# A hybrid encoder block in float32 pieces on one core: memory pools in another order, and tiles at multiples of 128 bytes

## The chip, the core and the metric

The kernel runs on one core of a Trainium2 chip. Its engines have a queue of instructions each: TensorE (PE, with the loading of the stationary operand, "PEld", as a queue that runs beside its matmuls), VectorE (DVE), ScalarE (ACT), GpSimd (POOL) and SyncE (SP), which issues all of this kernel's DMA transfers. The on-chip memory has 128 partitions; a tile is a stretch of bytes at the same address in each of them. The metric is the device time in microseconds (us) of one execution; lower is better.

## What is computed

One layer of a residual block over 1024 frames of 1024 values, and a last RMS norm. Group A is a gated linear recurrence in chunks of 64 frames (4 heads), group B a short gated convolution.

```python
h = rmsnorm(x, norm_gain[l])
proj = jnp.einsum('bsd,dc->bsc', h, w_in[l])          # 1024 x 1024 times 1024 x 4096
q, f_logit, i_in, z_a, u, gate_b, gate_c, z_b = jnp.split(proj, splits, axis=-1)
f = lb + (1.0 - lb) * jax.nn.sigmoid(f_logit.astype(jnp.float32))
o_a = hgrn2_chunkwise(q.reshape(hs), jnp.log(f).reshape(hs), (1.0 - f).reshape(hs), i_in.reshape(hs))
o_a = grouped_rmsnorm(o_a.reshape(bsz, s, D_HGRN), hgrn_norm_gain[l], HGRN_HEADS) * jax.nn.silu(z_a)
y_b = gate_b * causal_depthwise_conv(gate_c * u, conv_w[l])
o_b = grouped_rmsnorm(y_b, conv_norm_gain[l], CONV_GROUPS) * jax.nn.silu(z_b)
x = x + jnp.einsum('bsc,cd->bsd', jnp.concatenate([o_a, o_b], axis=-1), w_out[l])
return rmsnorm(x, final_norm_gain)
```

## The kernel before

**Matmuls.** Every large operand is split into a high part in float32r and a low part, the rest (lines 153 to 155, 301 to 315 and 662 to 664: a cast on ScalarE, a subtraction on VectorE). A product of two such operands is three matmuls: high by high, high by low, low by high. A matmul has a stationary operand of 128 x 128 and a moving one of 128 x 512.

**Stages.** First the value projection (lines 233 to 240, tiles `pv`), for two halves of the frames: stationary is a slice of x in XH or XL, moving are the weights of block k. For k below 4 these weights stand in XH and XL too (line 159), for k from 4 on in tiles `wvh` and `wvl` of the pools hip and lop (lines 161 and 162). Then 14 pairs of weight blocks (line 291): the first two pairs with 8 plain products each (tile `p`), the other 12 with 7 products each, by a Strassen-like scheme (tiles `pa`, `pb`, `pd`, `pe`). `product` (lines 335 to 343) issues 12 matmuls: stationary is a slice of the weights' high or low part (`hB`, `lB`, `hT`, `lT`, in the pools hip and lop), moving is a slab of XH or XL:

```python
pe.mm(ps, wh_[:, c], XH[:, a, k, :], start=(first and k == 0), stop=False, **more)
pe.mm(ps, wh_[:, c], XL[:, a, k, :], start=False, stop=False, **more)
pe.mm(ps, wl_[:, c], XH[:, a, k, :], start=False, stop=(last and k == 3), **more)
```

Last comes the output projection (`out_mms`, lines 794 to 804, tile `po`), in two halves of the output's columns: stationary is the mixed result in XH or XL, moving are the output weights. In the first half six of the eight blocks of weights stand in hip and lop (`woh`, `wol`, line 747) and two in XH and XL; in the second half all stand in XH and XL (line 743). The last tile is done in two pieces of 256 columns.

**Order.** All five queues are written by hand. A counter of the large matmuls (class `Stream`) places the other engines' work and the small float32 matmuls between them: scores and state updates of the recurrence (lines 477, 478, 491, 493, 494), the convolution's norm (602, 609), transposes (212, 681). So each engine's order is fixed by the code.

**Memory.** A pool takes its place when it is opened, in the order of lines 93 to 99; inside `const`, tiles follow one another in the order in which they are made, each rounded up to 32 bytes. `const` stands first and holds XH, XL, `vo` (values and later results), `mb`, `ident`, `mask` and the score tiles `sc`, with small tiles between them; the other pools begin where it ends.

Of the kernel before, what the change touches and what calls it, by code (L numbers as in the profile page):

```python
# [9 lines left out]
F32 = mybir.dt.float32  # L10
# [6 lines left out]
P = 128  # L17
# [3 lines left out]
NT = S // P  # L21
# [67 lines left out]
def hybrid_block(ctx: ExitStack, tc: tile.TileContext, xT, x, wv, wpair, wout, cols, fgain, out):  # L89
    nc = tc.nc  # L90
    A, V, G, T = nc.scalar, nc.vector, nc.gpsimd, nc.tensor

    const = ctx.enter_context(tc.tile_pool(name="const", bufs=1))
    hip = ctx.enter_context(tc.tile_pool(name="hip", bufs=NHL))
    lop = ctx.enter_context(tc.tile_pool(name="lop", bufs=NHL))
    rawp = ctx.enter_context(tc.tile_pool(name="rawp", bufs=6))
    tmp = ctx.enter_context(tc.tile_pool(name="tmp", bufs=8))
    qk = ctx.enter_context(tc.tile_pool(name="qk", bufs=2))
    sm = ctx.enter_context(tc.tile_pool(name="sm", bufs=2))
    dram = ctx.enter_context(tc.tile_pool(name="dram", bufs=2, space=bass.MemoryType.DRAM))  # L100
    psa = ctx.enter_context(tc.tile_pool(name="psa", bufs=1, space=PSUM))
# [17 lines left out]

    XH = const.tile([P, 7, 4, W], F32R, name="XH")  # L120
    XL = const.tile([P, 7, 4, W], F32R, name="XL")
    rst = const.tile([P, NT], F32, name="rst")
    vo = const.tile([P, NT, W], F32, name="vo")
    mb = const.tile([P, 4, S], F32, name="mb")
    col = const.tile([P, NCOL], F32, name="col")
    epsc = const.tile([P, 1], F32, name="epsc")
    ones = const.tile([P, 1], F32, name="ones")
    zeros = const.tile([P, 1], F32, name="zeros")
    ident = const.tile([P, P], F32, name="ident")

    pa = [bank_a(t, f"pv{t}") for t in range(4)]
    V.memset(zeros, 0.0)
# [110 lines left out]
        A.activation(vo[:, 4 * hf + t, :], p_, AF.Copy, scale=rst[:, 4 * hf + t:4 * hf + t + 1])  # L243


    mask = const.tile([P, P], F32, name="mask")
    G.memset(mask, 1.0)
    G.affine_select(out=mask, in_=mask, pattern=[[1, P]], compare_op=ALU.is_ge, fill=0.0, base=0,
                    channel_multiplier=-1)
# [1 line left out]
    G.memset(bones, 0.0)  # L251
    G.memset(bones[0:64, 0:1], 1.0 / 64)
    G.memset(bones[64:128, 1:2], 1.0 / 64)
    NS = 3
    scbuf = [const.tile([P, P], F32, name=f"sc{i}") for i in range(NS)]
    for s_ in scbuf:
        G.memset(s_, 0.0)

# [141 lines left out]
    def head(h):  # L400
# [71 lines left out]
        def scores(pr):  # L472
# [7 lines left out]
            pe.at(2, lambda: A.copy(kts[pr], psc[:, 1]),  # L480
                  lambda: V.copy_predicated(scbuf[(h * NT + pr) % NS], mask.bitcast(I32), psc[:, 0]))  # L481

        def combine(pr):
# [3 lines left out]
            vp = vo[:, pr, h * P:(h + 1) * P]  # L487
            sc, state = scbuf[(h * NT + pr) % NS], states.get(pr)
            po = psb.tile([P, 2, P], F32, tag="ps", name=f"po{n_}")
# [272 lines left out]
    for g, (n, step) in enumerate(products):  # L762
        if n == npair - 1:
            i = ORDER.index(step)
# [163 lines left out]
```

## Time and profile before

| | |
|---|---|
| device time, median of 3 runs | 470.25 us (469.73 to 570.84) |
| device time of the profiled execution | 469.7 us |
| its span, first to last instruction | 468.0 us |
| PE busy | 460.7 us (98%), 2200 matmuls |
| weight loads busy | 380.8 us |
| DVE, ACT, POOL busy | 326.6, 230.9, 101.8 us |
| moved by DMA | 40.83 MB |

The table is of one profiled execution. Matmuls overlap: each shows 0.39 to 0.48 us in the warm stretches, while a new one starts every 0.23 us or so. Their starts, not their durations, tell the pace.

### The profile page before, as it was taken

What the parts mean: (1) busy time and instruction counts of PE and PEld (TensorE: products, weight loads), DVE (VectorE), ACT (ScalarE), POOL (GpSimd) and SP (SyncE); (2) the same over time, 40 slices, a digit from 0 to 9 for tenths busy, and PEclk for the clock granted to TensorE, in tenths of its full rate; (3) what the DMA queues carried; (4) which work ended last, traced back from release to release, by engine and by line L of the source; (5) the groups of instructions that cost most, each with busy time, mean ns of one, the idle gap of its engine ahead of it and who ended that gap; (6) DMA issues with size and microseconds to landing.
All of it is one profiled execution on the core that took longest, in us unless ns stands there. A gap on an engine that the chain in (4) does not pass through costs nothing. (4 is left out here: it accounts for less than half of the span.)

```text
span 468.0 us, 6245 instructions
## 1 busy us (share of the span) xinstructions
PE 460.7 (98%) x2200; PEld 380.8 (81%) x2200; DVE 326.6 (70%) x593; ACT 230.9 (49%) x553; POOL 101.8 (22%) x92
## 2 busy tenths in 40 slices
PE   8999999999999999999999999999999999999995
PEld 7888888888888888888888888878888888888884
DVE  3668677989967789658799468798367796423333
ACT  5977415474454554454443545454646744314223
POOL 1100000005520053410326210326333343220000
PEclk9999999999999999999999999999999999999999
DMA  8990211120023020022020212020004228101442
GB/s 257 396 377 12 84 47 44 22 67 25 22 91 91 24 67 25 23 91 90 22 69 24 66 48 91 22 87 27 25 24 140 85 93 276 59 2 68 152 162 91
DMA packets 22031, 40.83 MB, mean 87 GB/s; under 512 B 2736, under 2 KB 2800, under 8 KB 22000
## 3 DMA queue, kind: packets, MB, share of 16 engines
q1 hardware_dynamic: 22000, 40.43, 26.2%
q8 instruction: 17, 0.28, 0.3%
q14 instruction: 14, 0.11, 0.1%
HBM read 36.19 MB, written 4.23 MB: 86 GB/s over the span
## 5 line engine op out<-in xcount | busy, mean ns | idle before, releaser
L314 DVE TENSOR_TENSOR lT<-T,hT 128x512 fp32r<-128x512 f32 x48 | 32.5, 677 | 32.8 <-ACT hT L313 32.5
L449 POOL TENSOR_TENSOR kh<-kh,ei 128x512 f32<-128x512 f32 x8 | 11.7, 1469 | 137.7 <-DVE ei L448 137.7
L60 PE MATMUL pb<-XH,lT 128*128 128x512 f32 x96 | 39.2, 408 | 0.0
L60 PE MATMUL pb<-XL,hT 128*128 128x512 f32 x96 | 38.7, 403 | 0.0
L60 PE MATMUL pb<-XH,hT 128*128 128x512 f32 x96 | 38.0, 396 | 0.0
L509 ACT COPY vo<-po 128x128 f32<-128x128 f32 x32 | 8.5, 266 | 54.6 <-DVE st L507 41.8
L313 ACT CAST hB<-B 128x512 fp32r<-128x512 f32 x44 | 27.6, 629 | 11.2 <-issue 11.1
L60 PE MATMUL po<-XH 128*128 128x512 f32 (+1 forms) x88 | 32.7, 372 | 0.0
L60 PE MATMUL po<-XH,XL 128*128 128x512 f32 (+1 forms) x88 | 32.7, 372 | 0.0
L60 PE MATMUL po<-XL,XH 128*128 128x512 f32 (+1 forms) x88 | 32.6, 370 | 0.0
L314 DVE TENSOR_TENSOR lB<-B,hB 128x512 fp32r<-128x512 f32 x44 | 32.2, 732 | 0.2 <-ACT hB L313 0.2
L313 ACT CAST hT<-T 128x512 fp32r<-128x512 f32 x48 | 28.4, 591 | 4.3 <-DVE T L305 4.3
L448 DVE RECIPROCAL ei<-e 128x128 f32<-128x128 f32 x32 | 29.5, 931 | 0.0
L60 PE MATMUL p<-XH,hB 128*128 128x512 f32 x64 | 25.3, 396 | 0.0
L60 PE MATMUL p<-XL,hB 128*128 128x512 f32 x64 | 25.3, 396 | 0.0
L60 PE MATMUL p<-XH,lB 128*128 128x512 f32 x64 | 25.3, 396 | 0.0
L60 PEld LDWEIGHTS pb<-XL,hT 128*128 128x128 f32 x96 | 18.0, 188 | 4.5 <-issue 0.3
L60 PEld LDWEIGHTS pb<-XH,hT 128*128 128x128 f32 x96 | 18.1, 188 | 4.1
L481 DVE COPY_PREDICATED sc<-mask,psc 128x128 f32<-128x128 int32 x32 | 9.6, 300 | 16.8 <-ACT kt L480 16.6
L60 PEld LDWEIGHTS pb<-XH,lT 128*128 128x128 f32 x96 | 18.1, 189 | 3.3
L60 PE MATMUL pe<-XL,hT 128*128 128x512 f32 x48 | 19.7, 410 | 0.0
L844 DVE TENSOR_TENSOR r<-po,xo 128x512 f32<-128x512 f32 (+1 forms) x9 | 5.7, 633 | 19.9 <-PE po L60 19.9
(217 smaller groups left out, 1367.8 us busy)
## 6 DMA issues: line engine op xcount, KB each, us to landing
B<-wpair SPq DMA_DIRECT2D x56, 256.0 KB, 2.6
wo<-wout SPq DMA_DIRECT2D x16, 256.0 KB, 3.0
xo<-x SPq DMA_DIRECT2D x16, 256.0 KB, 3.4
out<-y SPq DMA_DIRECT2D x16, 256.0 KB, 2.3
wv<-wv SPq DMA_DIRECT2D x8, 256.0 KB, 7.2
x<-xT SPq DMA_DIRECT2D x8, 256.0 KB, 6.2
vo<-x SPq DMA_DIRECT2D x4, 512.0 KB
mb<-xT SPq DMA_DIRECT2D x8, 256.0 KB, 5.9
```

The costliest lines, as they stand in the source:

```text
L60: self.T.matmul(*args, **kw)
L313: A.copy(hi, src)
L314: pe.at(5, lambda: V.tensor_tensor(lo, src, f32(hi), op=ALU.subtract))
L448: pe.at(9 + gap * i, lambda c0=i * P: V.reciprocal(eis[0][:, c0:c0 + P], e[:, c0:c0 + P]))
L449: pe.at(10 + 4 * gap - 3, lambda: G.tensor_tensor(kh, kh, eis[0], op=ALU.mult), lambda: G.tensor_tensor(ev[:, :, 0, :], ev[:, :, 0, :], ei ...
L481: lambda: V.copy_predicated(scbuf[(h * NT + pr) % NS], mask.bitcast(I32), psc[:, 0]))
L509: A.copy(vp, po[:, 0])
L844: V.tensor_tensor(r, po[:, c0:c1], xr[:, c0:c1], op=ALU.add)
```

## The change

Two things are put in another order: the pools (`const` is opened after hip, lop, rawp, tmp and qk instead of before them) and the tiles inside `const` (the large ones first, the small ones behind them; `ident`, `mask` and the three `sc` tiles move up).

```diff
-    const = ctx.enter_context(tc.tile_pool(name="const", bufs=1))
+
     hip = ctx.enter_context(tc.tile_pool(name="hip", bufs=NHL))
     lop = ctx.enter_context(tc.tile_pool(name="lop", bufs=NHL))
     rawp = ctx.enter_context(tc.tile_pool(name="rawp", bufs=6))
     tmp = ctx.enter_context(tc.tile_pool(name="tmp", bufs=8))
     qk = ctx.enter_context(tc.tile_pool(name="qk", bufs=2))
+    const = ctx.enter_context(tc.tile_pool(name="const", bufs=1))
     sm = ctx.enter_context(tc.tile_pool(name="sm", bufs=2))
...
     XL = const.tile([P, 7, 4, W], F32R, name="XL")
-    rst = const.tile([P, NT], F32, name="rst")
     vo = const.tile([P, NT, W], F32, name="vo")
     mb = const.tile([P, 4, S], F32, name="mb")
+    ident = const.tile([P, P], F32, name="ident")
+    mask = const.tile([P, P], F32, name="mask")
+    NS = 3
+    scbuf = [const.tile([P, P], F32, name=f"sc{i}") for i in range(NS)]
+    rst = const.tile([P, NT], F32, name="rst")
     col = const.tile([P, NCOL], F32, name="col")
...
-    ident = const.tile([P, P], F32, name="ident")
...
-    mask = const.tile([P, P], F32, name="mask")
...
-    NS = 3
-    scbuf = [const.tile([P, P], F32, name=f"sc{i}") for i in range(NS)]
```

The addresses in the two built programs, in bytes within a partition, and the offset of each from a multiple of 128:

| tiles | before | offset | after | offset |
|---|---|---|---|---|
| XH, XL | 384, 57728 | 0, 0 | 74112, 131456 | 0, 0 |
| hip (high parts) | 151232 to 163520 | 64 | 384 to 12672 | 0 |
| lop (low parts) | 163520 to 175808 | 64 | 12672 to 24960 | 0 |
| rawp, tmp, qk | 175808 to 224960 | 64 | 24960 to 74112 | 0 |
| vo, mb | 115104, 131488 | 32, 32 | 188800, 205184 | 0, 0 |
| ident, sc | 148128, 149280 | 32, 32 | 221568, 222592 | 0, 0 |
| mask | 148736 | 0 | 222080 | 0 |
| sm (`kt`, `st`, `dec`) | 225216 to 229312 | 64 | the same | 64 |

The instructions of all five queues, their order and their operands are the same in both programs, and so is which buffer of a pool each tile gets.

## Rows read from the trace of the kernel before

**Rows 1.** From the page: busy time of TensorE's two sides and VectorE, and granted clock.
```profile
PE 460.7 (98%) x2200; PEld 380.8 (81%) x2200; DVE 326.6 (70%) x593; ACT 230.9 (49%) x553; POOL 101.8 (22%) x92
PEclk9999999999999999999999999999999999999999
```
**Rows 2.** Who waited for whom, matmuls, then weight loads: us in total, times, longest.
```profile
PE pv L138 <- DVE epsc L133: 1.0, 1, 1.0
PE pv L60 <- ACT XH L179: 0.5, 1, 0.5
...
PEld pb L60 <- issue: 0.5, 3, 0.2
```
**Rows 3.** Timeline, the end: start, us taken, engine, line, what.
```profile
461.97 0.28 PE L60 MATMUL po<-XH,XL 128*128 128x256 f32 x1
...
464.83 0.37 SPq L866 DMA_DIRECT2D out<-y  x1
```
**Rows 4.** Timeline of TensorE's matmuls: first product, and the one after 192.
```profile
52.11 0.40 PE L60 MATMUL p<-XH,hB 128*128 128x512 f32 x1
...
96.91 0.40 PE L60 MATMUL pb<-XH,hB 128*128 128x512 f32 x1
```
**Rows 5.** The same, output projection's second half: first, and the one after 168.
```profile
418.24 0.40 PE L60 MATMUL po<-XH 128*128 128x512 f32 x1
...
456.34 0.28 PE L60 MATMUL po<-XH 128*128 128x256 f32 x1
```
**Rows 6.** The same, value projection, k below 4: one, and the 14th after it.
```profile
13.73 0.39 PE L60 MATMUL pv<-XL,XH 128*128 128x512 f32 x1
...
16.90 0.39 PE L60 MATMUL pv<-XH 128*128 128x512 f32 x1
```
**Rows 7.** The same, value projection, k of 4 and more: first, and the 41st after it.
```profile
18.26 0.40 PE L60 MATMUL pv<-wvh,XH 128*128 128x512 f32 x1
...
27.66 0.40 PE L60 MATMUL pv<-wvh,XL 128*128 128x512 f32 x1
```
**Rows 8.** Busy time by stretch: from and to, length, engines, granted clock, DMA, GB/s.
```profile
core 0: us, PE busy (x) PEld busy (x) DVE busy (x) ACT busy (x) POOL busy (x), PEclk, DMA share, GB/s
13.70:17.00 3.30, 3.30 (x16) 2.72 (x15) 1.42 (x3) 2.96 (x7) 0.00 (x0) 1.00 1.05 409
52.00:97.00 45.00, 45.00 (x195) 36.26 (x194) 35.18 (x58) 19.33 (x35) 0.00 (x0) 1.00 0.13 35
90.00:150.00 60.00, 60.00 (x289) 49.34 (x288) 52.05 (x97) 32.19 (x74) 15.43 (x12) 1.00 0.17 50
```
**Rows 9.** Timeline of TensorE around small matmuls, then their groups: busy us, mean ns.
```profile
129.14 0.38 PE L491 MATMUL po<-vo,kt 128*128 128x128 f32 x2
129.36 0.39 PE L494 MATMUL po<-vo,sc 128*128 128x128 f32 x2
129.50 0.48 PE L60 MATMUL pb<-XH,lT 128*128 128x512 f32 x1
129.82 0.39 PE L60 MATMUL pd<-XH,hB 128*128 128x512 f32 x1
...
L494 PE MATMUL po<-vo,sc 128*128 128x128 f32 x64 | 12.4, 275 | 0.0
L491 PE MATMUL po<-vo,kt 128*128 128x128 f32 x56 | 10.7, 273 | 0.0
L681 PE MATMUL pt<-ident,vo 128*128 128x128 f32 x32 | 4.8, 272 | 0.0
```
**Rows 10.** Groups of instructions by line: the split's subtraction into lop and into XL.
```profile
L155 DVE TENSOR_TENSOR wvl<-wv,wvh 128x512 fp32r<-128x512 f32 x4 | 2.8, 692 | 3.7 <-ACT wvh L154 3.7
L155 DVE TENSOR_TENSOR XL<-wv,XH 128x512 fp32r<-128x512 f32 x4 | 2.8, 690 | 4.7 <-ACT XH L154 4.7
```
**Rows 11.** Timeline: a low part on VectorE, and the load of it as weights.
```profile
176.00 0.63 DVE L314 TENSOR_TENSOR lT<-T,hT 128x512 fp32r<-128x512 f32 x1
...
183.01 0.19 PEld L60 LDWEIGHTS pb<-XH,lT 128*128 128x128 f32 x1
```

## What I predict

> **What bounds the kernel now.** The page comes first: of 468.0 us the matmul side of TensorE is busy 460.7, VectorE 326.6, and the granted clock is full in all 40 slices [rows 1]. A busy share can hide waiting, so the second view is the list of what TensorE's two sides waited for. Both rows of the matmul side lie in the first 6 us, and of the weight loads none waits more than 0.2 us after that [rows 2]. So from about 6 us to the last matmul at 461.97 [rows 3] the matmuls are issued as closely as the engine takes them, and the time is the sum of their distances from start to start. I write "step" for that distance. The third view is therefore the timeline of TensorE alone, of which only starts are read. Durations there are 0.39 to 0.40 us everywhere, overlap, and tell little.
>
> The step is not the same in all stages, although each stage shown here runs the same matmul (128 rows, 128 weights, 512 moving columns, float32r):
> - the products, tile `p`: 52.11 to 96.91 is 44.80 us over 192 matmuls, 233.3 ns [rows 4];
> - the second half of the output projection: 418.24 to 456.34 is 38.10 us over 168 matmuls, 226.8 ns [rows 5];
> - the value projection, k below 4: 13.73 to 16.90 is 3.17 us over 14, 226.4 ns [rows 6];
> - the value projection, k of 4 and more: 18.26 to 27.66 is 9.40 us over 41, 229.3 ns [rows 7].
>
> Now put addresses beside these. At 226 to 227 both operands lie in XH and XL, at a multiple of 128 bytes. At 229 the moving operand is `wvh`/`wvl` from hip and lop, 64 bytes off a multiple of 128, and the stationary one is aligned. At 233 the stationary operand is the one 64 off and the moving one is aligned. In code, products and output projection are alike: lines 341 to 343 and 802 to 804 issue three matmuls with the stationary operands a, a, b and the moving ones c, d, c, in long runs into one bank. Load by the other engines doesn't explain the difference: in 13.7 to 17 ScalarE is busy 2.96 of 3.30 us and the DMA engines all the time, at 226.4; in 52 to 97 ScalarE is busy 43% of the time and DMA 13%, at 233.3 [rows 8]. What is left is where the operands lie, and the change moves exactly that.
>
> **The change, part by part.** No instruction is added, removed or moved: on all five engines the order and the operands are those of before, so each term is a changed duration. All 512-column tiles come to multiples of 128.
>
> Stationary operands of the products. There are 2 x 8 x 12 + 12 x 7 x 12 = 1200 of these matmuls. 85 of them stand right behind a group of small matmuls (32 of scores, 32 of combine, 8 + 8 of the convolution's norm, 5 of the gate's transposes); the one in the rows takes 0.32 us to the next start [rows 9], and no aligned example exists in the products. The other 1115 go from 233.3 to 226.8: 6.5 ns each, 7.25 us. The 85 give between 0 and the same 6.5 ns, 0 to 0.55 us; I take the middle, 0.3. Together 7.55.
>
> Moving operands. 96 matmuls of the value projection (2 halves, 4 values of k, 4 tiles, 3 each) and 144 of the output projection's first half (8 tiles, 6 values of k, 3 each) read a moving tile that is 64 off: 229.3 - 226.8 = 2.5 ns each, 0.6 us.
>
> Small float32 matmuls. The records of lines 477, 478, 491, 493, 494, 602 and 681 whose operand gets a new offset are 64 + 32 + 56 + 56 + 64 + 64 + 32 = 368. They start 0.11 us apart [rows 9], and no aligned one is in the trace. Below: nothing. Above: the nearest row that prices a misplaced stationary operand, 6.5 ns each, 2.4 us. I stay near the lower end with 0.4 us, because their means of 272 to 275 ns don't part by the offset: in line 494 and line 681 the stationary tile is 32 off, in line 491 it is 64 off.
>
> VectorE, ScalarE and GpSimd. The split's subtraction takes 690 ns into aligned XL and 692 into `wvl` [rows 10]. So offsets cost these engines nothing that shows, and I set them to 0; were 1% lost there, it would lie under TensorE, since VectorE has 7.95 of 60 us free even in 90 to 150 [rows 8].
>
> DMA. Raw, x and y tiles are written or read at new offsets; no row has an aligned transfer. Only two places are not covered: the 0.5 us in which the first matmul waits for XH [rows 2] and the stores behind the last matmul [rows 3]. I bound this by plus or minus 0.5 us and take 0.
>
> Does a faster TensorE find its operands? The tightest weights that I found are `lT` of pair 5's last product: ready at 176.63 (176.00 + 0.63), first loaded at 183.01, 6.38 us early [rows 11]. A product of 12 steps becomes 0.08 us shorter, so such a lead of about two products loses 0.2 us. Nothing new is waited for.
>
> Sum: 7.55 + 0.6 + 0.4 = 8.55 us. The profiled execution took 469.7 us (span 468.0 and 1.7 around it), which gives 461.2. The median of the runs shown is 470.25, 0.55 above it, which gives 461.7. I forecast **461.6 us**, 1.8% below. With every unknown at its lower end the gain is 7.25 + 0.6 = 7.85 less 0.5, so 462.9; at the upper end 7.8 + 0.6 + 2.4 + 0.5 = 11.3, so 459.0.
>
> One rule speaks against all of this. In the Trainium skill, page SBUF — State Buffer, section Specifications (TRN2), the memory's lines are 16 bytes, and only crossing to a new line costs. Every address here is a multiple of 32 before as after, so by that rule the sum is 0 and the time stays at 470. The steps of 233.3 and 226.8 ns [rows 4, 5] are a difference that the rule doesn't provide for, unless something other than the address makes it.
>
> **The rivals.**
> *No change.* The 233.3 ns would belong to the products as such: traffic of other engines, the banks, the kind of accumulation. For it: no product in the trace has an aligned stationary tile, so the comparison is between stages. Against it: the same matmul pattern in both stages, and the busiest stretch has the shortest step [rows 6, 8]. 470.0 us, chance 0.13.
>
> *Height, not offset.* Before, hip and lop lie at 151 to 176 thousand bytes, above XH and XL (up to 115 thousand). If a high address were what is slow, the products would gain 7.55 all the same, since their weights move to the bottom, but XL moves up to 131 to 189 thousand. The `xl` weights of the value and output projections, a third of 576 matmuls, would then lose 192 x 6.5 ns = 1.25 us. Gain 6.3 to 6.9: 463.6 us. Against it: only that 64 bytes explain both 229 and 233 more simply. Chance 0.10.
>
> *A supply that doesn't follow.* VectorE is busy 52.05 of 60 us in 90 to 150 [rows 8]; if a chain of it and ScalarE there set the pace instead, half of the gain would go: 466 us. The leads above speak against it. Chance 0.04.
>
> *Slower: the two streams meet.* With all tiles at one offset, the weights and the moving columns of a product would be read in the same phase. If that made them collide, the products would go up instead of down; with as much again as the present difference, 1200 x 6.5 ns = 7.8 us, the time is 478. To be slower by over 2% (9.4 us) it takes 7.8 ns a matmul. Against it: in the value projection below k = 4 and in the second half of the output projection both streams are at one offset already, and these steps are the shortest [rows 5, 6]. Chance 0.03.
>
> **How the numbers follow.** The forecast's own case has 0.70, from 459.0 to 462.9. Taking in the height rival and the lost half of the gain gives 0.84; the range is 459.3 to 466.5, and leaves out no change and slower. A change of 2%, about what a measurement of this kernel can tell from no change, is 9.4 us, a time of 460.85. My sum lies 0.75 us on the near side of that; it is passed only if the small matmuls gain over 1 us or DMA helps. Faster by over 2%: 0.14, all out of the forecast's case. Slower by over 2%: 0.03, the streams that meet. Within 2%: 0.83.
>
> **What would show it.** Right: the 192 matmuls of tile `p` are 226 to 227 ns apart instead of 233.3; those with `wvh` and `woh` 227 instead of 229; the steps of [rows 5, 6] stay; nothing new appears in what TensorE waits for; and the span shrinks by as much as these steps add up to. Wrong: `p` stays at 233 (something else in the products); `pv<-XH` and `po<-XH` rise on the `XL` weights (height); `p` falls and waits appear (supply); `p` rises (the streams meet). The small matmuls' 0.11 us decides between 461 and 459.

## The result, and the profile after

The changed kernel takes **463.9 us** (median of 4 runs, 463.16 to 464.61); the kernel before 469.9 us, the median of its three fast runs (469.73 to 470.25), as a fourth of 570.84 us is a slow one and is left out. The ratio is 0.987, with a 95% interval of 0.985 to 0.989: a gain of 6.0 us or 1.3%, inside the predicted range and below 2%. The profiled execution took 464.6 us, the longest of the four, and that of the kernel before 469.7, so the sums below are made against the 5.1 us between these two (span 468.0 to 462.9).

The page of the changed kernel, the rows that answer to [rows 1] and the span:

```profile
span 462.9 us, 6245 instructions
...
PE 454.9 (98%) x2200; PEld 380.5 (82%) x2200; DVE 326.1 (70%) x593; ACT 230.4 (50%) x553; POOL 101.3 (22%) x92
...
PEclk9999999999999999999999999999999999999998
```

The number of instructions is the same, the granted clock is full until the last matmul is done, as before, and VectorE, ScalarE and GpSimd are busy within 0.5 us of what they were. Only TensorE's matmul side became shorter.

What TensorE's two sides waited for in the changed kernel (us in total, times, longest):

```profile
PE pv L142 <- DVE epsc L137: 1.0, 1, 1.0
PE pv L60 <- ACT XH L183: 1.0, 1, 1.0
...
PE pss L603 <- DVE sc L482: 0.3, 1, 0.3
...
PEld pss L603 <- DVE sc L482: 0.7, 1, 0.7
```

The first two are those of [rows 2]; that for XH is 0.5 us longer. The last two are new, and one place (below).

The timeline of TensorE in the changed kernel at the borders of the stages (start, us taken, line, what), to be set beside [rows 3 to 5]:

```profile
52.06 0.39 PE L60 MATMUL p<-XH,hB 128*128 128x512 f32 x1
...
95.58 0.39 PE L60 MATMUL pb<-XH,hB 128*128 128x512 f32 x1
...
368.08 0.39 PE L60 MATMUL po<-woh,XH 128*128 128x512 f32 x1
...
413.14 0.39 PE L60 MATMUL po<-XH 128*128 128x512 f32 x1
...
451.22 0.28 PE L60 MATMUL po<-XH 128*128 128x256 f32 x1
...
456.86 0.28 PE L60 MATMUL po<-XH,XL 128*128 128x256 f32 x1
```

From these starts and those of before (the first product of the Strassen part, as I call the 12 pairs with 7 products, starts at 96.91 there [rows 4], the output projection at 372.70), stage by stage in us:

| stage | before | after | gain | predicted |
|---|---|---|---|---|
| start of the first large matmul | 5.31 | 5.74 | -0.43 | 0 |
| value projection (and first waits) | 46.80 | 46.32 | 0.48 | 0.24 |
| products of tile `p`, 192 matmuls | 44.80 | 43.52 | 1.28 | 1.25 |
| Strassen part, 1008 product matmuls and the small ones | 275.79 | 272.50 | 3.29 | 6.70 |
| output projection, first half | 45.54 | 45.06 | 0.48 | 0.36 |
| output projection, second half | 38.10 | 38.08 | 0.02 | 0 |
| last matmul starts at | 461.97 | 456.86 | 5.11 | 8.55 |

The step in tile `p` went from 233.3 to 43.52 / 192 = 226.7 ns, as predicted (226.8). The Strassen part, where most of the matmuls are, gave half of what was predicted. Two questions follow: is the offset from a multiple of 128 really the cause, and where did the other half go?

### The profile page after: what moved, and what is told of

Read it like the earlier page. It is cut to its first block, busy times and chain, and to the rows that moved or that the text cites. A ratio compares the mean times of both kernels' runs of the same rounds, so it can differ in the third digit from the quotient of the medians.

```text
span 462.9 us, 6245 instructions
## 1 busy us (share of the span) xinstructions
PE 454.9 (98%) x2200; PEld 380.5 (82%) x2200; DVE 326.1 (70%) x593; ACT 230.4 (50%) x553; POOL 101.3 (22%) x92
```

## Experiments: which addresses matter

Each ratio below is against runs of the kernel before on the same chip. Their medians were 468.6 to 470.3 us on the two chips used, so times of different experiments compare to 1 or 2 us only; the steps are what is read.

Three theories. **Offset**: each operand pays for not lying at a multiple of 128, wherever the other lies (the prediction's picture). **Height**: a stationary operand far up in the partition is slow. **Difference**: only the distance between stationary and moving operand counts, modulo some power of two. The first and the third fit the two kernels above. Height already has something against it: the change moves XL up to 131456 to 188800, and the second half of the output projection, with a third of its weights there, stays at 226.7 ns. The experiments place the tiles otherwise and change nothing else: the instructions and their order stay. Read is the step in tile `p` (stationary in hip and lop, moving in XH and XL), and, as its counterpart, the first 41 steps of the value projection for k of 4 and more, which no other matmul interrupts (stationary in XH and XL, moving in hip and lop). In the changed kernel the latter are:

```profile
18.48 0.39 PE L60 MATMUL pv<-wvh,XH 128*128 128x512 f32 x1
...
27.77 0.39 PE L60 MATMUL pv<-wvh,XL 128*128 128x512 f32 x1
```

That is 226.7 ns, against 229.3 before [rows 7].

**1. The layout of before, hip and lop 64 bytes lower.** Three small tiles of `const` become one, so that hip lands at 151168, still high; what lies between these tiles and sm moves along, and a pad in sm keeps the rest in place.

```diff
 (kernel before)
+    sm.tile([P, 16], F32, tag="pad", name="smpad", bufs=1)
...
-    epsc = const.tile([P, 1], F32, name="epsc")
-    ones = const.tile([P, 1], F32, name="ones")
-    zeros = const.tile([P, 1], F32, name="zeros")
+    eoz = const.tile([P, 3], F32, name="eoz")
+    epsc, ones, zeros = eoz[:, 0:1], eoz[:, 1:2], eoz[:, 2:3]
```

> The layout of before, with three one-column tiles of const put into one, so that hip, lop, rawp, tmp and qk begin 64 bytes lower (hip at 151168 instead of 151232, offset 0 instead of 64). XH and XL stay at the bottom, hip and lop stay at the top, sm stays at 64, vo, mb and ident stay off. Offset theory: the 192 matmuls of tile p are 226.8 ns apart instead of 233.3, and the time is that of the changed kernel within 1 us, 463 to 465 us. Height theory: hip lies as high as before, so p stays at 233 ns and the time at 470 us.

Measured: 464.3 us, ratio 0.989 (0.987 to 0.992). Its timeline, the first product and the one after 192:

```profile
52.27 0.39 PE L60 MATMUL p<-XH,hB 128*128 128x512 f32 x1
...
95.79 0.39 PE L60 MATMUL pb<-XH,hB 128*128 128x512 f32 x1
```

43.52 us, 226.7 ns, as in the changed kernel, though the weights lie where they lay before but for 64 bytes. So the order of the pools gives nothing by itself, and height falls.

**2. The changed kernel, every large tile 64 bytes further.** They all lie 64 off a multiple of 128, hip at 448 and XH at 74176.

```diff
 (changed kernel; eoz as in 1)
+    padp = ctx.enter_context(tc.tile_pool(name="padp", bufs=1))
+    padp.tile([P, 16], F32, name="pad")
     hip = ctx.enter_context(tc.tile_pool(name="hip", bufs=NHL))
```

> The layout of the changed kernel with 64 bytes in front of hip: every 512-column tile, XH and XL too, is 64 off a multiple of 128 (small tiles put together to make room; sm unchanged). Offset theory: stationary and moving operands are both off, so p goes to 233.3 ns or above, about 236 if the two prices add, and the second half of the output projection, 226.8 before, goes up with it; the time is 472 to 478 us. Relative theory (only a difference between the two streams' offsets costs): p at 226.8 ns and 464 us.

Measured: 463.3 us, ratio 0.988 (0.986 to 0.991). Its timeline:

```profile
50.71 0.39 PE L60 MATMUL p<-XH,hB 128*128 128x512 f32 x1
...
94.23 0.39 PE L60 MATMUL pb<-XH,hB 128*128 128x512 f32 x1
```

Again 43.52 us. No large tile is at a multiple of 128, and the gain is whole. So the offset theory falls, and with it the prediction's explanation of the pace; the difference theory had this right.

**3. Only XH, XL and what follows them moved by 64 bytes.** hip stays at 384; the difference has the size of before, with the other sign.

```diff
 (changed kernel; eoz as in 1)
+    const.tile([P, 16], F32, name="pad")
     XH = const.tile([P, 7, 4, W], F32R, name="XH")
```

> The layout of the changed kernel with 64 bytes between qk and XH: hip and lop aligned, XH, XL, vo, mb, ident and sc 64 off. In the products the stationary operand is aligned and the moving one off; in the projections the stationary operand is off. Offset theory with a price for each operand: p at 229.3 ns (the moving price, 2.5 ns); output projection's second half (both off) about 236, its first half with woh (stationary off, moving aligned) 233; about 464 + 1200 x 2.5 ns + 576 x 7 ns = 471 us. Relative theory: p at 233 ns, output's second half at 226.8.

Measured: 466.9 us, ratio 0.994 (0.991 to 0.997). Its timeline:

```profile
17.51 0.39 PE L60 MATMUL pv<-wvh,XH 128*128 128x512 f32 x1
...
27.08 0.40 PE L60 MATMUL pv<-wvh,XL 128*128 128x512 f32 x1
...
51.73 0.39 PE L60 MATMUL p<-XH,hB 128*128 128x512 f32 x1
...
95.67 0.39 PE L60 MATMUL pb<-XH,hB 128*128 128x512 f32 x1
...
414.47 0.39 PE L60 MATMUL po<-XH 128*128 128x512 f32 x1
...
452.55 0.28 PE L60 MATMUL po<-XH 128*128 128x256 f32 x1
```

43.94 us, 228.9 ns: not 226.7, though the stationary operand lies as in the changed kernel; and the 41 steps of the value projection rise to 233.3 ns. Before, these two numbers stood the other way round (233.3 and 229.3) [rows 4, 7]. It is the sign of the difference that tells them apart, not which stage it is. Neither theory had all of this: for tile `p` the offset theory's 229.3 was the better forecast, and the difference theory, which knew no sign, was wrong with 233. But the second half of the output projection, where both operands lie in XH and XL and both are 64 off, stays at 226.7 (38.08 us over 168), where the offset theory wanted 236. It does so in every kernel here, with XH at 0, 128, 160 or 192 modulo 256.

**4. The layout of before, hip, lop and the pools behind them 32 bytes higher.**

```diff
 (kernel before)
     ssl = const.tile([P, 1], F32, name="ssl")
+    const.tile([P, 8], F32, name="pad")
```

> The layout of before with 32 bytes more in const: hip, lop, rawp, tmp, qk and sm at an offset of 96 instead of 64, all else as before. If what counts is only whether an operand starts at a multiple of 128, p stays at 233 ns and the time at 470 us. If what counts is a multiple of 64, the step goes further up, by up to as much again (240 ns), and the time to as much as 478 us.

Measured: 471.0 us, ratio 1.004 (1.002 to 1.006). Its timeline:

```profile
53.24 0.39 PE L60 MATMUL p<-XH,hB 128*128 128x512 f32 x1
...
98.22 0.40 PE L60 MATMUL pb<-XH,hB 128*128 128x512 f32 x1
```

44.98 us, 234.3 ns, 1.0 more than before: a difference of 96 bytes is about as dear as one of 64.

**5. The changed kernel, XH 128 bytes higher.** A tile of 128 bytes that exists anyway is made ahead of XH; every large tile still begins at a multiple of 128.

```diff
 (changed kernel)
+    ssa = const.tile([P, NH, NT], F32, name="ssa")
     XH = const.tile([P, 7, 4, W], F32R, name="XH")
...
-    ssa = const.tile([P, NH, NT], F32, name="ssa")
```

> The layout of the changed kernel with the tile ssa (128 bytes) moved in front of XH: hip and lop as there, XH and XL 128 bytes further up, so that the two operands of a product differ by 128 modulo 256 (all runs so far at 226.8 ns had a difference that is a multiple of 256). If a multiple of 128 is enough, as the change's rule says: p at 226.8 ns and the time of the changed kernel, 464 us. If it takes a multiple of 256: p at 229 to 236 ns and 466 to 471 us.

Measured: 468.4 us, ratio 0.997 (0.996 to 0.999). Its timeline:

```profile
51.90 0.40 PE L60 MATMUL p<-XH,hB 128*128 128x512 f32 x1
...
96.53 0.39 PE L60 MATMUL pb<-XH,hB 128*128 128x512 f32 x1
```

44.63 us, 232.4 ns. So multiples of 128 are not what gives the gain: with all tiles at such multiples most of it is gone. In 1 the difference is 256 modulo 512, in the changed kernel 0, and both are quick; so, as far as these tell, the period is 256.

**6. The changed kernel, XH 32 bytes higher.** In the same way, with `rst` (32 bytes) ahead of XH.

```diff
 (changed kernel)
+    rst = const.tile([P, NT], F32, name="rst")
     XH = const.tile([P, 7, 4, W], F32R, name="XH")
...
-    rst = const.tile([P, NT], F32, name="rst")
```

> The layout of the changed kernel with the tile rst (32 bytes) moved in front of XH: in the products the stationary operand lies 32 bytes lower than the moving one (modulo 256), in the projections' parts with hip and lop 32 higher. With -64 the step was 229 ns and with +64 233 ns. If the price grows with the distance, p is between 226.8 and 229 ns, about 228, and the time 465 us; if any distance costs about the same, p is at 229 ns or more and the time 466 to 471 us. At either sign, a difference of the two streams' offsets costs; if 32 is free, p is at 226.8 ns.

Measured: 470.6 us, ratio 1.002 (1.000 to 1.003). Its timeline:

```profile
52.79 0.39 PE L60 MATMUL p<-XH,hB 128*128 128x512 f32 x1
...
97.59 0.39 PE L60 MATMUL pb<-XH,hB 128*128 128x512 f32 x1
```

44.80 us, 233.3 ns. The smallest difference that could be made costs the whole gain, and three times as much as 64 on the same side (3): the price does not grow with the distance.

All of it in one table. D is the address of the stationary operand less that of the moving one, modulo 256; in the value projection it has the other sign. The steps are from unrounded starts:

| kernel | D, tile `p` | step, ns | D, value projection, k of 4 and more | step of the first 41, ns |
|---|---|---|---|---|
| after, 1, 2 | 0 | 226.7 | 0 | 226.7 |
| before | 64 | 233.3 | -64 | 229.3 |
| 3 | -64 | 228.9 | 64 | 233.3 |
| 4 | 96 | 234.3 | -96 | 233.6 |
| 5 | 128 | 232.4 | 128 | 233.2 |
| 6 | -32 | 233.3 | 32 | 233.4 |

Where the two columns share a D (64, -64, 128) they agree within 0.8 ns, in different stages. The first half of the output projection, with the value projection's D in 144 of its matmuls, bears it out: 45.06 to 45.08 us at 0, 45.54 at -64, and 45.88 to 46.07 at 64, 128, -96 and 32.

## Experiments: where the other half of the gain went

In the Strassen part the matmuls can be sorted by their neighbours. Of its 1008 product matmuls 85 stand right behind a group of small ones, 85 right ahead of one, and 838 between two products. From the starts:

| matmuls | before, ns | after, ns | gain, us |
|---|---|---|---|
| 838 between products | 233.3 | 229.2 | 3.47 |
| 85 behind a group | 318.3 | 315.9 | 0.21 |
| 85 ahead of a group | 232.7 | 235.3 | -0.22 |
| small ones, in all | 33.42 us | 33.57 us | -0.15 |

The 838 come to 229.2 and not to 226.7. The timeline of the changed kernel around two groups shows how it goes (in brackets the idle time before, and who ended it):

```profile
179.27 0.38 PE L478 MATMUL psc<-qh,kh 128*128 128x128 f32 x2
179.49 0.27 PE L479 MATMUL psc<-ident,kh 128*128 128x128 f32 x1
179.52 0.48 PE L60 MATMUL pe<-XL,hT 128*128 128x512 f32 x1
179.83 0.39 PE L60 MATMUL pe<-XH,lT 128*128 128x512 f32 x1
...
181.68 0.39 PE L60 MATMUL pb<-XL,hT 128*128 128x512 f32 x1
182.37 1.05 PE L603 MATMUL pss<-bones,b 128*128 128x2 f32 x8 [0.31 <-DVE sc L482]
```

The matmul behind the first group takes 0.31 us to the next, and the 8 from 179.83 to 181.68 take 1.85 us, 231 ns each. Then the next group is there. So it is nearly everywhere: 73 of the 85 groups have only 7 or 8 products ahead of them. Sorted by their place behind the last group, the 838 show where the gain is:

| place behind the last group | matmuls | before, ns | after, ns |
|---|---|---|---|
| 2nd to 6th | 425 | 233.4 | 231.2 |
| 7th to 10th | 72 | 233.2 | 229.6 |
| 11th and later, and those ahead of the first group | 341 | 233.3 | 226.7 |

With more room the full gain is there; in the first places behind a group only a third of it. The two waits for `sc` above are also here: the norm's matmuls came so soon that VectorE's `sc` was 0.3 us late, and the matmul ahead took 695 ns; the other 84 of its kind average 229.8.

Two theories: the group by itself disturbs the pace of the matmuls behind it, or the other engines do, which read the group's result and fetch new operands at just that time. A third: the small matmuls' own operands, which lie in sm at 64, keep the gain away.

**7. A group that nobody reads, in the undisturbed stage.** In the changed kernel a small matmul is put behind 14 of the 16 products of tile `p`: float32 with `ident` in the first pair, float32r with a piece of XH in the second. No engine reads its result.

```diff
 (changed kernel)
+            if n or i not in (5, 6):
+                psd = psb.tile([P, 2, P], F32, tag="ps", name=f"dummy{n}_{i}")
+                a, b = (XH[:, A11, 0, :P], XH[:, A11, 1, :P]) if n else (ident, ident)
+                T.matmul(psd[:, 0], a, b, start=True, stop=True)
```

> The changed kernel with one extra small matmul (128 x 128, 128 columns, its result read by nobody) behind each plain product of the first two pairs: in pair 0 a float32 one (from the third product on), in pair 1 a float32r one. No other engine reads what it writes. If a group of small matmuls itself leaves the following large ones at a longer step (the changed kernel's products with groups between them start 229 to 236 ns apart instead of 227), then behind each dummy some 5 to 10 matmuls are at 229 to 236 ns before 227 comes back. If the other engines' reads of the groups' results are the cause, the step is 227 again from the second matmul behind a dummy on. The float32r dummy tells whether it is the two passes of float32.

Measured: 466.1 us in one run, with the added matmuls in it. Its timeline, from a float32 one to the next, and behind a float32r one:

```profile
59.01 0.38 PE L376 MATMUL dummy<-ident 128*128 128x128 f32 x2
59.15 0.48 PE L60 MATMUL p<-XH,hB 128*128 128x512 f32 x1
59.46 0.40 PE L60 MATMUL p<-XL,hB 128*128 128x512 f32 x1
...
61.77 0.39 PE L60 MATMUL p<-XH,lB 128*128 128x512 f32 x1
62.00 0.38 PE L376 MATMUL dummy<-ident 128*128 128x128 f32 x2
...
82.69 0.22 PE L376 MATMUL dummy<-XH 128*128 128x128 f32 x1
82.75 0.45 PE L60 MATMUL p<-XH,hB 128*128 128x512 f32 x1
83.03 0.39 PE L60 MATMUL p<-XL,hB 128*128 128x512 f32 x1
...
84.19 0.39 PE L60 MATMUL p<-XH,hB 128*128 128x512 f32 x1
...
85.32 0.39 PE L60 MATMUL p<-XH,lB 128*128 128x512 f32 x1
```

Behind the float32 matmul one step of 0.31 us, and then the 10 from 59.46 to 61.77 take 2.31 us, 231 ns each: the next group is there before 226.7 returns. Behind the float32r one the 5 from 83.03 to 84.19 average 232 ns, and the next 5, to 85.32, 226. So a single small matmul costs the matmuls behind it 5 x 5.3 = 27 ns or 10 x 4.3 = 43 ns beyond its own time and the one long step, without any other engine. In the Strassen part 838 x (229.2 - 226.7) = 2.1 us over 85 groups is 25 ns a group, of that size, and there too the pace is back by the 11th. The group by itself is enough as a cause; that the other engines add nothing is not shown.

**8. sm at a multiple of 128.** With `eoz` as in 1, the changed kernel's sm pool (`kt`, `st`, `dec`) comes to an offset of 0.

```diff
 (changed kernel)
-    epsc = const.tile([P, 1], F32, name="epsc")
-    ones = const.tile([P, 1], F32, name="ones")
-    zeros = const.tile([P, 1], F32, name="zeros")
+    eoz = const.tile([P, 3], F32, name="eoz")
+    epsc, ones, zeros = eoz[:, 0:1], eoz[:, 1:2], eoz[:, 2:3]
```

> The changed kernel with three one-column tiles of const put into one, so that the pool sm (kt, st, dec, rr) begins 64 bytes lower and its tiles are at multiples of 128 too; all else stays where it was. If the small matmuls' own operands at an offset of 64 make the long steps behind their groups, these go back to 227 and the time falls by up to 2 us, to 462 us. If not, the time is that of the changed kernel, 463.9 us, within 0.5.

Measured: 464.7 us, ratio 0.990 (0.988 to 0.992), not the 462 that the third theory wanted. The Strassen part takes 272.42 us (272.50 after), the 838 average 229.2 ns, the small ones 33.54 us. Nothing changes; the third theory falls.

**9. Fewer groups: scores behind the state update.** If the group is the cause, 61 groups instead of 85 should give back part of it. The scores of pair `pr + 2` are issued directly behind the state update of pair `pr` instead of half a step later.

```diff
 (changed kernel)
-                    pe.later(STEP // 2, lambda: scores(pr + 2))
-                pe.later(STEP, lambda: combine(pr + 1))
+                pe.later(STEP, lambda: both(pr + 1))
...
+        def both(pr):
+            combine(pr)
+            if pr < NT - 2:
+                scores(pr + 2)
...
-            pe.later(STEP + 4, lambda: combine(0))
+            pe.later(STEP + 4, lambda: both(0))
```

> The changed kernel with the scores of one pair of chunks issued directly behind the state update of another, instead of 8 large matmuls later: the same small matmuls, but one group per 16 large matmuls instead of two. If each group costs its following matmuls some 30 ns in all, 28 groups fewer save about 1 us: 462.9 us, and between groups the step comes back to 227. If the long steps belong to something that runs there anyway, the time stays at 463.9 us.

Measured: 471.2 us, ratio 1.005 (1.003 to 1.007): 7 us slower than the changed kernel. Its waits of TensorE that were not there before:

```profile
PE prr L614 <- ACT po L511: 2.5, 2, 1.6
PE pss L607 <- ACT po L511: 1.5, 3, 0.5
PE pt L686 <- ACT po L511: 1.2, 1, 1.2
```

There are 24 groups fewer, not the 28 expected, and no gain. The joined group takes both banks of the pool of small results in PSUM, the memory of the matmuls' results, at once, and the next small matmul has to wait until ScalarE has read one. These lines hold 5.2 us of the loss; the Strassen part is 279.22 us, 6.72 more than in the changed kernel. The matmuls between products, 886 now, fell from 229.2 to 228.4 ns all the same.

**10. The same, both results in one bank.**

```diff
 (kernel of 9)
         def both(pr):
-            combine(pr)
+            bank = psb.tile([P, 4, P], F32, tag="ps", name=f"pb{h}_{pr}")
+            combine(pr, bank[:, 0:2])
             if pr < NT - 2:
-                scores(pr + 2)
+                scores(pr + 2, bank[:, 2:4])
```

> As the run with joined groups, but the results of a joined group (state update and scores) share one PSUM bank, where they took both banks of their pool. If the 7 us that joining lost are waits for a bank, they go, and what 28 groups fewer save is left: 462 to 463.5 us. If joining itself puts the state chain or ScalarE behind, the time stays above 466 us.

Measured: 464.1 us, ratio 0.988 (0.986 to 0.990). Its waits of TensorE:

```profile
PE pv L60 <- ACT XH L183: 1.6, 1, 1.6
...
PE pv L142 <- DVE epsc L137: 1.0, 1, 1.0
...
PE pss L608 <- DVE sc L482: 0.4, 1, 0.4
```

The waits for the banks are gone, so they were what made 9 slow. The matmuls between products are at 228.5 ns and the Strassen part takes 272.14 us, 0.36 less than in the changed kernel. That is the sign that the theory wants, but the expected 462 to 463.5 us was missed, and as a whole this kernel can't be told from the changed one. The products' steps became 2.4 us shorter in all, but the small matmuls took 35.64 us instead of 33.57: the long step behind a group (316 ns) only moves into the joined one. What fewer groups save beyond that is the 0.36 us.

## Why the prediction was right or wrong

**What bounds the kernel, and reading starts: right.** The last matmul starts 5.11 us earlier and the span shrinks by 5.1; the other engines' busy times stayed.

**The range was met in part by luck.** The forecast's own case went from 459.0 to 462.9, and 463.9 lies outside it. The range held it because it was stretched for two rivals, height (463.6) and half the gain lost to a late supply (466), and neither is what took the missing gain.

**The products' term: right per matmul where nothing interrupts, mis-sized as a whole.** The step that failed is "The other 1115 go from 233.3 to 226.8: 6.5 ns each, 7.25 us". The 192 of tile `p` did, with 1.28 us. The 923 others gave 3.47 - 0.22 = 3.25 us instead of 6.0, since behind each of the 85 groups the step stays at 231 or so for 5 to 10 matmuls (7) and most groups come 7 or 8 products after the last. The kernel before could not show this: at its pace of 233.3 a group left no trace in the matmuls behind, as the equal 233.3 in tile `p` and between groups tells. The aligned rows that I took the 226.8 from [rows 5, 6] come from stages without groups, and the price was carried to a stage with them.

**The term of the 85: nearly right**, 0.21 us for 0.3. **The small matmuls: wrong**, 0.4 us expected, -0.15 measured; the reading of their equal means by offset was the better guide, and 8 agrees. Of the 8.55 us these three miss 2.75 + 0.1 + 0.55 = 3.4, which is the whole gap to 5.1; the smaller rows of the stage table cancel out.

**Moving operands: right in size.** The value projection for k of 4 and more came from 229.3 to 226.7, the output projection's first half gave 0.48 us for 0.36.

**VectorE, ScalarE, DMA: right at 0** within what shows. The first large matmul starts 0.43 us later, because ScalarE began its first piece of x at 4.96 instead of 4.54 us, released last by the transfer of `col`. Neither that nor most of the value projection's length goes with the layout: the kernels of 9 and 10 have the same addresses there, and take 47.32 and 44.91 us for that stage. From the first product to the last matmul the four kernels at D = 0 (after, 1, 2, 8) take 404.7 to 404.8 us, against 409.86 before, while their first products start anywhere from 50.71 to 52.27 us. So the differences among their profiled executions, 463.2 to 464.7 us, arise ahead of the products; of the 6.0 us between the medians, what exceeds the 5.1 is not traced.

**"What is left is where the operands lie": right. "64 off a multiple of 128": wrong as a cause.** It is the difference of the two operands' addresses modulo 256 (2, 3, 5, 6). In the kernel before both pictures fit every row, because wherever both operands were at a multiple of 128 they were in XH and XL, and so at D = 0. The change helps since it brings all large tiles to 128 modulo 256, which is more than it says, and that is luck: with XH at the next multiple of 128 its rule was kept as well, and the time was 468.4 us (5).

**The rivals.** No change falls by the result. The Trainium skill, page SBUF — State Buffer, section Specifications (TRN2), gives lines of 16 bytes, with a penalty for each crossing to a new one. By that alone the addresses here would all cost the same, and the measurement goes beyond it: all large tiles in 1 to 6 lie at multiples of 32, and the step ranges from 226.7 to 234.3 ns by address alone. Height falls by 1. The supply that doesn't follow is there in one place of 0.46 us (the 695 ns step) and nowhere else. The streams that meet are the reverse of what is so: one offset for both is the quick case, and any other tested costs 2.2 to 7.6 ns.

**What stays open.** What inside TensorE makes the step depend on the two addresses isn't visible in the records. Differences other than those in the table weren't tried, nor other types and sizes of large matmuls. Nor is it shown why 5 to 10 matmuls pass before the pace is back behind a small one, and whether another address for the small operands than that of 8 would change it.

## What to carry to other kernels

Where TensorE issues matmuls like these back to back, compare the start addresses of stationary and moving operand modulo 256 and make them equal, with padding if need be; moving hip and lop by 64 bytes (1) did here what the new order of all pools did. Price such a gain only from rows with the same neighbours: a step measured in an undisturbed run of matmuls isn't reached where small ones come after every seven or eight. Before an address is named as the cause, move everything together by the same amount: that tells an absolute offset from a relative one in one run.

## What was not expected of the hardware

- The step of a 512-column float32r matmul depends on D modulo 256: 226.7 ns at 0, 228.9 to 229.3 at -64, and 232.4 to 234.3 at 32, -32, 64, 96, -96 and 128. It is not symmetric at 64 (64 against -64) and does not grow with the distance (-32 is dearer than -64).
- One small matmul of 128 columns, whose result nobody reads, slows the 5 (float32r) or 10 (float32) large ones behind it to 231 or 232 ns at D = 0. At D = 64, where the step is 233.3 anyway, no such mark is seen.
- The offset of the small float32 matmuls' operands in sm (64 or 0) has no price that shows: 33.57 and 33.54 us for all of them (8).
